# Value products in reverse order, matmuls of zeros at the start and in ten waits, a pinned norm broadcast, pinned weight splits and GpSimd subtractions in halves

## The chip, the cores and the metric

The kernel runs on one core of one Trainium2 chip. A core has TensorE (PE, matrix products, with weight loads shown apart as PEld), VectorE (DVE), ScalarE (ACT), GpSimd (POOL) and a queue on SyncE (SP) that issues the DMA transfers here. Each engine works through its own instructions strictly in the order in which they were emitted and waits where an operand is not there. The metric is the device time of one execution in microseconds (us); lower is better.

## The reference

Two transformer layers over two streams of 256 tokens, the context stream (s=0) and the latent stream (s=1), with model width 1024. Each layer is a half-step SwiGLU feed-forward stage, a token-mixing stage and another half-step feed-forward stage, and each stage reads a modulated RMS norm of the streams:

```
def modulate(h, g, shift, scale):
    return rms_norm(h, g) * (1 + scale) + shift

def swiglu(h, wi, wo):
    gt, up = jnp.split(h @ wi, 2, axis=-1)
    return (jax.nn.silu(gt) * up) @ wo

for l in range(DEPTH):            # DEPTH = 2
    x  = x  + HALF * mod_l[2] * swiglu(modulate(x,  ...), ffn1_wi[l], ffn1_wo[l])
    xc = xc + HALF * mod_c[2] * swiglu(modulate(xc, ...), ffn1_wi[l], ffn1_wo[l])
    y_l, y_c = token_mix(modulate(x, ...), modulate(xc, ...), w_in[l], ...)
    x  = x + mod_l[5] * (y_l @ w_out[l])
    x  = x + HALF * mod_l[8] * swiglu(modulate(x, ...), ffn2_wi[l], ffn2_wo[l])
    # the context stream likewise, in the first layer only
```

`token_mix` projects the normed streams with one input matrix and splits the columns among three groups of heads: A, a bidirectional mLSTM; B, six heads of latent attention; C, six heads of windowed attention with a sink logit per head. An attention head is a softmax over score tiles and a product of the probabilities with the values. The outputs of the groups are joined and projected by `w_out`.

## The kernel before, in words

All large products are made nearly exact in a fast format: a weight `w` is split into a high part (`ACT`, `AF.Copy` into float32r) and a low part (`w` minus the high part, on DVE or on POOL, `split`, L241 to L251), a stream likewise, and `mm3` (L237) adds three products for each pair of tiles. Other products (statistics, broadcasts, attention scores from full floats, value products) are plain float32; in the trace each of those shows as two records.

The feed-forward stages (`ffn`, L443) take 22 column blocks `j`; `up` makes gate and up products over eight row tiles `kt`, `down` (L574) the output rows. At the very start, in `norm_first` (L394), the statistics of the inputs are taken, and `ada_block` (L304) makes the eight blocks of the first modulation, one for each `kt`; a row tile of the normed stream (`modulate`, L377) needs its block. In between stages a `Norm` object (L98) carries the norm of a stream: `sq` squares each finished row tile on ACT (L111) and adds the squares on POOL (L115), `stats` sums over partitions with one-column products and raises to the power -1/2 on POOL (`rsqrt`, L375), `bcast` spreads the result over partitions with two small products, and `mods` applies it, row tile by row tile: DVE L383, then ACT L386 and DVE L387 for even row tiles, ACT L390, L391 and POOL L392 for odd ones.

The mixing stage (`mix`, L1182) is cut into some hundred small units (generators): projections (`chunk`, `proj`; names k1, k2, cq, o, v, q1, q2), attention tiles (`attend`, L607), mLSTM heads, the output projection. A table `PLAN` gives each group of units a place and a step, the units are sorted by it, and `run` starts `add` of them per round and keeps up to `width` of them active (`CFG`). Tables `CHP` and `OPT` choose which engine does a split or a copy. Within all of this a list scheduler with its own model of times decides the final order on each engine.

In `attend`, a tile takes scores into PSUM, the row maximum (DVE L629 or L632, with L633 for the sink), the exponential (ACT L637), the sum with the sink's term (DVE L643), the reciprocal (L644), the normalisation (POOL L651, DVE L649 or ACT L647), four transposes (PE L657), their copies, and for the last tile of a pair of heads the value product (PE L671), two heads beside each other in the array.

Of the kernel before, what the change touches and what calls it, by code (L numbers as in the profile page):

```python
# [10 lines left out]
F32 = mybir.dt.float32  # L11
F32R = mybir.dt.float32r
AF = mybir.ActivationFunctionType
ALU = mybir.AluOpType
# [23 lines left out]
def dper(nj):  # L38
# [18 lines left out]
]  # L57
CFG = [(2, 9), (1, 10)]
CHP = [
    {"k1": 1, "cq": 1, "o": 1, "k2": 0, "v": 1, "q1": 1, "q2": 0},  # L60
    {"k1": 1, "cq": 0, "o": 1, "k2": 0, "v": 0, "q1": 0, "q2": 1},
]
OPT = [
# [3 lines left out]
     "rbcq": 1, "sqfi": 2},  # L67
# [14 lines left out]
]  # L82
MODS = {0: (0, 0, 0, 2, 1, 1, 0, 0), 2: (0, 0, 0, 1, 1, 1, 1, 1), 3: (0, 0, 0, 2, 1, 1, 0, 0)}
# [14 lines left out]
class Norm:  # L98
# [19 lines left out]
    def stats(self):  # L118
        b, p = self.b, self.begin()
        self.R = b.ps((P, 258), "R1" if self.s else "R0")  # L120
        for tt in range(2):
            for t in self.sqs:
                b.mm(self.R[:, 256 + tt:257 + tt], t[:, tt * P:(tt + 1) * P], b.ones, t is self.sqs[0],
                     t is self.sqs[-1])
        self.r = b.sm(2, "sn")
        b.rsqrt(self.r, self.R[:, 256:258], 1.0 / D, 2)
        b.phase = p
# [14 lines left out]
class Builder:  # L142
    def __init__(self, tc, a, es):
# [17 lines left out]
        self.layer = 2  # L161

# [71 lines left out]
    def mm(self, out, lhsT, rhs, start, stop):  # L234
        self.nc.tensor.matmul(out, lhsT, rhs, start=start, stop=stop)  # L235
# [6 lines left out]
    def split(self, raw, alloc, shape, pool=False):  # L242
# [10 lines left out]
    def setup(self):  # L253
# [18 lines left out]
        nc.vector.memset(self.ones, 1.0)  # L272
        self.nhalf = c.tile([P, 16], F32, name="nhalf")
# [103 lines left out]
    def modulate(self, l, i, s, kt, R, hh, hl):  # L377
# [7 lines left out]
        if kt % 2 == 0:  # L385
            nc.scalar.activation(hh[kt][:, u], t, AF.Identity, bias=sh)  # L386
            nc.vector.scalar_tensor_tensor(hl[kt][:, u], t, sh, hh[kt].bitcast(F32)[:, u],  # L387
                                           op0=ALU.add, op1=ALU.subtract)
        else:
            nc.scalar.activation(t, t, AF.Identity, bias=sh)  # L390
            nc.scalar.activation(hh[kt][:, u], t, AF.Copy)  # L391
            nc.gpsimd.tensor_tensor(hl[kt][:, u], t, hh[kt].bitcast(F32)[:, u], op=ALU.subtract)  # L392

    def norm_first(self):  # L394
# [6 lines left out]
        qs = []  # L401
        for s in range(2):
# [7 lines left out]
        for s in range(2):  # L410
            self.phase = "norm000"
            u = slice(s * 256, s * 256 + 256)
            for tt in range(2 * s, 2 * s + 2):
                for k in range(2):
                    self.mm(st[tt], qs[s][:, k, tt % 2 * P:(tt % 2 + 1) * P], self.ones, k == 0, k == 1)
# [1053 lines left out]
```

## Time and profile before

| | |
|---|---|
| time, median of 3 runs (lowest to highest) | 1780.37 us (1778.57 to 1781.23) |
| the profiled execution: its own time | 1779.1 us |
| its span, from first to last instruction | 1777.4 us |
| PE busy | 1735.6 us, 98% of the span |
| PEld, DVE, ACT, POOL busy | 84%, 68%, 40%, 17% |
| mean granted clock of TensorE | 0.994 |
| DMA | 252.34 MB, mean 142 GB/s |

PE is busy nearly all the time. Two things are to be read of it: where it waits, and at which clock it works. The profile lists the clock that was granted, 1.00 being the upper of its two levels (2.4 GHz) and 0.50 the lower (1.2 GHz). A matmul's listed duration includes its pipeline, so the pace of a series is read from the starts.

### The profile page before, as it was taken

How to read it: one execution, taken by the hardware profiler on the slowest of the kernel's cores; microseconds unless marked ns; L12 is line 12 of the kernel's file. 1: busy time of each engine (PE TensorE's matmuls, PEld its weight loads, DVE VectorE, ACT ScalarE, POOL GpSimd, SP SyncE). 2: the span in 40 equal slices, each digit the busy share in tenths (PEclk: the TensorE clock that was granted, in tenths of full speed). 3: DMA queues.
4: the chain of work that ended last, by engine and by line, in shares of the span. 5: the costliest groups of instructions: out<-in, count | busy, mean ns of one | idle time of the engine just before them, and what ended most of it. 6: DMA issues, size and time to landing. Idle time of an engine off the chain costs nothing. (4 is left out here: it accounts for less than half of the span.)

```text
span 1777.4 us, 27225 instructions
## 1 busy us (share of the span) xinstructions
PE 1735.6 (98%) x10048; PEld 1494.9 (84%) x10048; DVE 1215.6 (68%) x2836; ACT 705.0 (40%) x1340; POOL 309.2 (17%) x350
## 2 busy tenths in 40 slices
PE   7999999999999999999999999999999999999999
PEld 5788888899977799888888898888888887699999
DVE  5699687957778856986853469785334588755555
ACT  3422222235566664222222353222322566554443
POOL 2100000025344680000000030000000466340000
PEclk9999999999999999999999999999999999999999
DMA  8656455632110145574633346654223241045654
GB/s 335 208 185 223 150 191 182 213 97 81 61 37 25 48 140 197 183 237 147 197 103 91 118 135 210 210 170 154 82 76 123 69 126 45 23 129 162 210 158 150
DMA packets 99590, 252.34 MB, mean 142 GB/s; under 512 B 12289, under 2 KB 16769, under 8 KB 98433
## 3 DMA queue, kind: packets, MB, share of 16 engines
q1 hardware_dynamic: 99456, 250.60, 43.5%
q8 instruction: 79, 1.29, 0.3%
q14 instruction: 55, 0.44, 0.1%
HBM read 249.51 MB, written 1.05 MB: 141 GB/s over the span
## 5 line engine op out<-in xcount | busy, mean ns | idle before, releaser
L246 ACT ACTIVATE w<-raw 128x1024 fp32r<-128x1024 f32 (+2 forms) x366 | 344.7, 944 | 573.9 <-PE tr L235 232.6
L250 DVE TENSOR_TENSOR w<-raw,w 128x1024 fp32r<-128x1024 f32 (+1 forms) x330 | 354.2, 1074 | 204.5 <-ACT w L246 202.9
L235 PE MATMUL sc<-h,w 128*128 128x512 f32 (+1 forms) x1428 | 355.3, 365 | 0.0
L235 PE MATMUL sc<-big,w 128*128 128x256 f32 (+1 forms) x1488 | 328.8, 340 | 1.8 <-ACT big L386 1.1
L235 PE MATMUL tr<-h,w 128*128 128x512 f32 (+1 forms) x1128 | 298.2, 373 | 1.2 <-DVE h L387 0.6
L235 PEld LDWEIGHTS sc<-h,w 128*128 128x128 f32 x1428 | 251.1, 190 | 44.0 <-issue 1.6
L235 PEld LDWEIGHTS sc<-big,w 128*128 128x128 f32 x1488 | 245.0, 191 | 32.0 <-issue 1.8
L235 PE MATMUL tr<-big,w 128*128 128x256 f32 (+1 forms) x1128 | 243.3, 326 | 0.0
L235 PEld LDWEIGHTS tr<-h,w 128*128 128x128 f32 x1128 | 204.9, 190 | 38.3 <-DVE h L387 0.8
L235 PE MATMUL ps<-h,w 128*128 128x256 f32 (+1 forms) x1404 | 216.3, 312 | 0.6 <-DVE x L436 0.6
L235 PEld LDWEIGHTS ps<-h,w 128*128 128x128 f32 x1404 | 195.4, 191 | 16.1 <-DVE x L436 0.9
L248 POOL TENSOR_TENSOR w<-raw,w 128x1024 fp32r<-128x1024 f32 (+2 forms) x36 | 84.1, 2340 | 688.4 <-ACT w L246 686.1
L235 PEld LDWEIGHTS tr<-big,w 128*128 128x128 f32 x1128 | 182.5, 191 | 17.8
L235 PE MATMUL ps<-big,w 128*128 128x512 f32 (+1 forms) x864 | 185.5, 372 | 0.7 <-DVE x L436 0.7
L352 DVE CUSTOM_DVE_ANT_0 hold<-a,a 128x512 f32<-128x512 f32 x256 | 177.7, 694 | 4.0 <-DMA a<-ada_t 4.0
L352 DVE CUSTOM_DVE_ANT_0 a<-a,a 128x512 f32<-128x512 f32 x256 | 175.8, 687 | 3.7
L235 PEld LDWEIGHTS ps<-big,w 128*128 128x128 f32 x864 | 153.6, 188 | 29.3 <-DVE x L436 1.0
L235 PE MATMUL ps<-w,h 128*128 128x256 f32 (+1 forms) x1152 | 169.3, 300 | 7.7 <-POOL h L392 2.1
L235 PEld LDWEIGHTS ps<-w,h 128*128 128x128 f32 x1152 | 151.2, 195 | 15.9 <-POOL h L392 2.3
L467 DVE TENSOR_TENSOR a<-a,tr 128x512 f32<-128x512 f32 (+1 forms) x90 | 54.3, 603 | 149.3 <-ACT a L466 78.3
L466 ACT ACTIVATE a<-sc 128x512 f32<-128x512 f32 (+1 forms) x91 | 48.3, 531 | 271.4 <-PE sc L235 266.4
L436 DVE SCALAR_TENSOR_TENSOR x<-ps,gate,x 128x256 f32<-128x256 f32 x150 | 68.2, 479 | 67.2 <-PE ps L235 66.9
(253 smaller groups left out, 1582.5 us busy)
## 6 DMA issues: line engine op xcount, KB each, us to landing
raw<-wi SPq DMA_DIRECT2D x176, 512.0 KB, 4.2
a<-ada_t SPq DMA_DIRECT2D x256, 256.0 KB, 4.6
raw<-wo SPq DMA_DIRECT2D x128, 320.0 KB, 3.0
raw<-w_out SPq DMA_DIRECT2D x24, 512.0 KB, 3.4
big<-ada_s SPq DMA_DIRECT2D x8, 1024.0 KB, 10.9
raw<-wo SPq DMA_DIRECT2D x8, 512.0 KB, 3.6
raw<-win_q SPq DMA_DIRECT2D x8, 512.0 KB, 4.1
a<-crow SPq DMA_DIRECT2D x12, 256.0 KB, 6.4
```

Source lines behind the costliest of these rows:

```text
L235: self.nc.tensor.matmul(out, lhsT, rhs, start=start, stop=stop)
L246: nc.scalar.activation(h, raw, AF.Copy)
L248: nc.gpsimd.tensor_tensor(l, raw, h.bitcast(F32), op=ALU.subtract)
L250: nc.vector.tensor_tensor(l, raw, h.bitcast(F32), op=ALU.subtract)
L352: nc.vector.tensor_tensor_reduce(out=w if s else junk, in0=w, in1=self.cb[s, hf], scale=1.0, scalar=0.0, op0=ALU.mult, op1=ALU.add, accum_ ...
L436: self.nc.vector.scalar_tensor_tensor(xs, ps, self.gate[l][:, s, i, d:d + 1], xs, op0=ALU.mult, op1=ALU.add)
L466: nc.scalar.activation(sg, pg, AF.Silu)
L467: nc.vector.tensor_tensor(sg, sg, pu, op=ALU.mult)
```

## The change

What it does, in the code:

- **Zeros at the start.** `norm_first` issues products of zeros (128x512, plain float32) into a bank that nobody reads: six at the very start, two behind the statistics of stream 0, one of 256 columns behind those of stream 1 (`FIRST`).
- **Zeros in ten waits.** `pad` issues products of zeros into the bank that the next real product overwrites (or adds to), at ten places (`PADS`): behind the statistics of two norms, ahead of one row tile of the first feed-forward stage of layer 1, and ahead of the transposes of seven attention tiles, where they read the sum of the exponentials and so start when it is there. All 29 issues of zeros are nine at the start, two of 256 columns behind statistics, two in the feed-forward stage and 16 of 128 columns.
- **Pinned order.** In the norms between stages, the next ordinary product may not be moved ahead of the broadcast (`first`); the zeros behind the statistics come ahead of it. The high parts of the k2 weights may not be moved ahead of the last ACT step of stream 0's norm (`late`).
- **Halves.** Where POOL makes the low part of a weight, it does so in two halves along the row tiles: 36 instructions become 74, with some splits moved between DVE and POOL (`CHP`).
- **The sink's sum** (L643) becomes a `tensor_scalar` with the sink's term as its per-partition scalar.
- **Value products and gate transposes** go through their tiles in reverse order.
- **Tables** `PLAN`, `CFG`, `OPT`, `CHP` get new entries, which reorder units of both mixing stages.

```
+FIRST = {0: (512,) * 6, 1: (512, 512), 2: (256,)}
+PADS = {"at0C0201": 384, "at0C1000": 512, "at0C1010": 384, "at1C0000": 768, "at1C1011": 128, "at1C1201": 256,
+     "at1C1210": 384, "r010": 384, "r100": 256, "up1007": 384}
...
-    {"k11": (-1, 4.1), "k10": (0, 1), "n1": (2, 0), "k20": (1.8, 0.6), "k21": (3.7, 0.6), "B10": (13, 2), "cq": (9,
+    {"k11": (-1, 4.1), "k10": (0, 1), "n1": (2, 0), "k20": (8, 0.9), "k21": (4.6, 0.6), "B10": (13, 2), "cq": (9,
...
         b.rsqrt(self.r, self.R[:, 256:258], 1.0 / D, 2)
+        b.pad(self.R[:, 0:256], f"r{self.l}{self.i}{self.s}", True, last, whole=True)
...
     def mm(self, out, lhsT, rhs, start, stop):
-        self.nc.tensor.matmul(out, lhsT, rhs, start=start, stop=stop)
+        i = self.last = self.nc.tensor.matmul(out, lhsT, rhs, start=start, stop=stop)
+        if self.first is not None:
+            self.behind(i, self.first)
+            self.first = None
...
+    def pad(self, out, key, start=False, after=None, x=None, whole=False):
+        n = PADS.get(key, 0)
+        w = out.shape[1]
+        if n and start:
+            n = max(1, n // w) * w
+        for k in range(0, n, w):
+            m = min(w, n - k)
+            i = self.nc.tensor.matmul(out[:, 0:m], self.zero.to_broadcast([P, P]), (self.zero if x is None else
+                                      x[:, 0:1]).to_broadcast([P, m]), start=start, stop=whole)
+            if after is not None:
+                self.behind(i, after)
+        return n > 0
...
-        nc.scalar.activation(h, raw, AF.Copy)
+        i = nc.scalar.activation(h, raw, AF.Copy)
+        if late:
+            self.behind(i, self.after["a"])
         if pool:
-            nc.gpsimd.tensor_tensor(l, raw, h.bitcast(F32), op=ALU.subtract)
+            m = shape[1] // 2
+            for v in (slice(0, m), slice(m, shape[1])):
+                nc.gpsimd.tensor_tensor(l[:, v], raw[:, v], h.bitcast(F32)[:, v], op=ALU.subtract)
...
+        warm(0)
         for s in range(2):
...
+            warm(1 + s, last)
             for tt in range(2 * s, 2 * s + 2):
                 self.mm(R[:, tt * P:(tt + 1) * P], r[:, tt:tt + 1].to_broadcast([P, P]), self.ident, True, True)
...
                                         nx[0].bcast()
+                                        self.first = self.last
...
-                nc.vector.tensor_tensor(st[:, 2:3], st[:, 2:3], st[:, 3:4], op=ALU.add)
+                nc.vector.tensor_scalar(st[:, 2:3], st[:, 2:3], st[:, 3:4], None, op0=ALU.add)
...
             for kt in range(nkt):
+                if kt == 0:
+                    self.pad(tr[:, 0, :], f"at{self.layer}{label[3]}{s}{heads[0]}{b}{qi}", True, None, st[:, 2:3], True)
                 nc.tensor.transpose(tr[:, kt, :], p[:, kt * P:(kt + 1) * P], self.ident)
...
-                for kt in range(nkt):
-                    for b2, h2 in enumerate(heads):
-                        nc.tensor.matmul(pv[64 * b2:64 * b2 + 64, :], V(kt, h2), pts[b2][kt // 2][:, kt % 2, :],
-                                         start=kt == 0, stop=kt == nkt - 1, tile_position=(0, 64 * b2))
+                for kt in reversed(range(nkt)):
+                    for b2 in (1, 0):
+                        nc.tensor.matmul(pv[64 * b2:64 * b2 + 64, :], V(kt, heads[b2]), pts[b2][kt // 2][:, kt % 2, :],
+                                         start=kt == nkt - 1, stop=kt == 0, tile_position=(0, 64 * b2))
```

**PE at the very start.** Before, these rows lead to the first product of the first feed-forward stage (sc_216 on h_4, row tile 0); `ps_189`, `ps_242` and `ps_286` are the modulation blocks 0, 1 and 2, the one-column products are statistics, the `ident,sn` products the broadcast.

```order
L316 MATMUL ps_189<-big_119,a_3_126 32x256 x8
L235 MATMUL hold_163<-ident,sn_165 128x128
L235 MATMUL sc_161<-ones,w_29_172 128x1 x2
L235 MATMUL sc_162<-ones,w_29_172 128x1 x2
L235 MATMUL ps_189<-sel,a_32_198 128x2 x2
L235 MATMUL hold_163<-ident,sn_165 128x128 x2
L316 MATMUL ps_242<-big_240,a_3_126 32x256 x8
L235 MATMUL ps_242<-sel,a_50_251 128x2 x2
L316 MATMUL ps_286<-big_284,a_3_126 32x256 x8
L235 MATMUL sc_216<-h_4_143,w_40_224 128x512
```

In the change the same place on PE reads as follows (`ps_169` takes the zeros; six more of them and the statistics of stream 0 stand ahead of these rows).

```order
L442 MATMUL ps_169<-a_27_168 128x512 x2
L349 MATMUL ps_202<-big_119,a_3_128 32x256 x8
L460 MATMUL sc_163<-ones,w_31_183 128x1 x2
L460 MATMUL sc_164<-ones,w_31_183 128x1
L242 MATMUL hold_165<-ident,sn_167 128x128 x2
L460 MATMUL sc_164<-ones,w_31_183 128x1
L442 MATMUL ps_169<-a_27_168 128x256
L242 MATMUL hold_165<-ident,sn_167 128x128 x2
L242 MATMUL ps_202<-sel,a_34_211 128x2 x2
L349 MATMUL ps_257<-big_255,a_3_128 32x256 x8
L242 MATMUL ps_257<-sel,a_52_266 128x2 x2
L242 MATMUL sc_230<-h_4_145,w_42_238 128x512
```

Block 2 no longer stands ahead of the first product: it comes behind the first twelve of them.

**PE at the end of the first feed-forward stage of layer 0.** Before, twelve `down` products (`ps_3465`, `ps_3496`) stand between the statistics of stream 0 and their broadcast, and six (`ps_3507`) behind it, ahead of the k1 projection. These rows are the last of the twelve and what follows.

```order
L235 MATMUL ps_3496<-big_3100,w_630_3192 128x256
L235 MATMUL ps_3496<-big_3101,w_629_3191 128x256
L235 MATMUL hold_3413<-ident,sn_3418 128x128 x2
L235 MATMUL ps_3507<-big_3100,w_629_3191 128x256
L235 MATMUL ps_3507<-big_3100,w_630_3192 128x256
```

In the change the zeros and the broadcast follow the statistics directly.

```order
L127 MATMUL hold_3429<-ones,a_652_3341 128x1
L127 MATMUL hold_3429<-ones,a_666_3417 128x1
L258 MATMUL hold_3429<-zero 128x256
L242 MATMUL hold_3429<-ident,sn_3434 128x128 x2
L242 MATMUL ps_3482<-big_3116,w_631_3207 128x256
```

All eighteen `down` products now stand between the broadcast and the k1 projection. The order at the two later boundaries (from layer 0 to layer 1, and into the mixing stage of layer 1) changes in the same way, the second of them without zeros.

**POOL in the mixing stage of layer 1.** The rows with `h_` are the last steps of stream 1's norm (L392, in the change L425), those with `sq_` powers of norms of heads.

```order
L392 TENSOR_TENSOR h_2502_12820<-a_2643_13448,h_2501_12819 128x256
L375 TENSOR_TENSOR sq_13453<-sq_13453,nhalf 128x2
L375 TENSOR_TENSOR sq_13479<-sq_13479,nhalf 128x6
L392 TENSOR_TENSOR h_2506_12824<-a_2650_13473,h_2505_12823 128x256
L232 TENSOR_TENSOR a_2645_13457<-a_2645_13457,sq_13479 128x576
```

In the change:

```order
L425 TENSOR_TENSOR h_2504_12874<-a_2637_13484,h_2503_12873 128x256
L408 TENSOR_TENSOR sq_13515<-sq_13515,nhalf 128x2
L425 TENSOR_TENSOR h_2508_12878<-a_2646_13509,h_2507_12877 128x256
L408 TENSOR_TENSOR sq_13583<-sq_13583,nhalf 128x6
L239 TENSOR_TENSOR a_2648_13519<-a_2648_13519,sq_13583 128x576
```

The last step of the norm now stands ahead of the 128x6 power.

## Rows read from the trace of the kernel before

**Rows 1.** Busy us (and instructions) of PE, PEld, DVE, ACT, POOL; granted clock; DMA.

```profile
390.00:404.00 14.00, 12.56 (x97) 11.58 (x96) 11.72 (x27) 9.26 (x23) 11.64 (x15) 1.00 0.43 141
404.00:411.00 7.00, 7.00 (x31) 7.00 (x31) 3.48 (x7) 2.78 (x8) 3.85 (x5) 0.51 0.22 77
...
547.50:551.00 3.50, 3.50 (x14) 1.93 (x14) 2.34 (x10) 3.03 (x11) 2.13 (x5) 0.52 0.02 7
...
1020.00:1035.50 15.50, 13.90 (x108) 12.89 (x108) 13.58 (x29) 10.70 (x28) 11.80 (x14) 1.00 0.30 99
1035.50:1039.00 3.50, 3.50 (x18) 3.50 (x18) 2.22 (x5) 1.51 (x5) 2.90 (x4) 0.51 0.50 147
...
1390.00:1428.00 38.00, 33.83 (x243) 31.27 (x241) 28.71 (x71) 23.79 (x60) 22.70 (x27) 1.00 0.23 72
1428.00:1431.50 3.50, 3.32 (x13) 2.95 (x14) 1.26 (x3) 2.37 (x7) 3.42 (x4) 0.51 0.57 185
...
1581.50:1585.50 4.00, 3.63 (x17) 3.36 (x18) 4.00 (x10) 3.94 (x11) 1.92 (x3) 0.57 0.09 33
```

**Rows 2.** PE in order of time at the start: start us, us, instructions merged, [idle before].

```profile
10.31 1.87 PE L235 MATMUL tr<-ones,w 128*128 128x1 f32 x8 [10.31 <-DVE w L409]
...
24.05 1.93 PE L316 MATMUL ps<-big,a 128*32 128x256 f32 x16
25.91 1.22 PE L235 MATMUL sc<-h,w 128*128 128x512 f32 x2
...
28.63 0.64 PE L235 MATMUL tr<-h,w 128*128 128x512 f32 x2
...
31.46 0.62 PE L316 MATMUL ps<-big,a 128*32 128x256 f32 x2
...
36.74 1.93 PE L316 MATMUL ps<-big,a 128*32 128x256 f32 x30
```

**Rows 3.** ACT in order of time at the start.

```profile
22.94 0.89 ACT L386 ACTIVATE h<-a,mod 128x256 fp32r<-128x256 f32 x2
```

**Rows 4.** PE, ACT and POOL in order of time, into the mixing stage of layer 0.

```profile
397.58 1.68 PE L235 MATMUL ps<-big,w 128*128 128x256 f32 x12
...
401.41 1.04 ACT L246 ACTIVATE w<-raw 128x1024 fp32r<-128x1024 f32 x1
...
404.76 6.63 PE L235 MATMUL ps<-w,h 128*128 128x304 f32 x26
...
407.65 1.41 POOL L392 TENSOR_TENSOR h<-a,h 128x256 fp32r<-128x256 f32 x2
```

**Rows 5.** PE in order of time, a broadcast right behind its statistics (end of layer 1's mixing).

```profile
1579.65 0.71 PE L235 MATMUL sc<-ident,sn 128*128 128x128 f32 x4 [1.04 <-POOL sn L375]
```

**Rows 6.** PE's waits from 1394 to 1436 us: total, times, longest.

```profile
PE ps L235 <- POOL h L392: 2.1, 1, 2.1
```

**Rows 7.** POOL in order of time, mixing stage of layer 1, first half.

```profile
1424.29 2.40 POOL L375 TENSOR_TENSOR sq<-sq,nhalf 128x6 f32<-128x6 f32 x1 [1.15 <-DVE sq L374]
```

**Rows 8.** DVE lines L643 and L633: duration ns min/median/max, first and last start.

```profile
L643 DVE TENSOR_TENSOR sa<-sa x36: 129/150/2075, 542.6 to 1546.9; 128x1 f32<-128x1 f32 x36
...
L633 DVE TENSOR_SCALAR sa<-sa,sink x36: 192/202/215, 534.9 to 1544.8; 128x1 f32<-128x1 f32 x36
```

**Rows 9.** POOL, DVE and PE in order of time, mixing stage of layer 1.

```profile
1506.98 2.34 POOL L248 TENSOR_TENSOR w<-raw,w 128x1024 fp32r<-128x1024 f32 x1
...
1507.26 2.08 DVE L643 TENSOR_TENSOR sa<-sa 128x1 f32<-128x1 f32 x1
...
1509.82 0.47 PE L235 MATMUL ps<-big,kSA 96*128 96x256 f32 x2 [1.16 <-DVE sa L633]
```

**Rows 10.** PE in order of time, mixing stage of layer 0.

```profile
546.38 0.63 PE L657 MATMUL tr<-ident,a 128*128 128x128 f32 x4 [1.48 <-DVE w L968]
```

**Rows 11.** The chain that ended last, in order of time: start us, us, what.

```profile
1494.89 0.86 PE sc L235 x2
```

**Rows 12.** PE's groups of instructions: busy us, mean ns, idle before.

```profile
L671 PE MATMUL ps<-a,big 128*64 128x256 f32 x240 | 40.0, 396 | 1.2 <-DVE a L224 0.6 <-DVE tot L1125 0.5
```

More of the change, by code (lines that the diff above doesn't have):

```diff
@@ L161, in __init__ @@
         self.layer = 2
+        self.last = self.first = None
+        self.after = {}
     def nm(self, s):
@@ L240, in mm3, with split @@
         self.mm(out, wh, xl, False, last)
-    def split(self, raw, alloc, shape, pool=False):
+    def split(self, raw, alloc, shape, pool=False, late=False):
         nc = self.nc
@@ L272, in setup @@
         nc.vector.memset(self.ones, 1.0)
+        self.zero = c.tile([P, 1], F32, name="zero")
+        nc.vector.memset(self.zero, 0.0)
         self.nhalf = c.tile([P, 16], F32, name="nhalf")
@@ L390, in modulate @@
             nc.scalar.activation(t, t, AF.Identity, bias=sh)
-            nc.scalar.activation(hh[kt][:, u], t, AF.Copy)
+            i = nc.scalar.activation(hh[kt][:, u], t, AF.Copy)
             nc.gpsimd.tensor_tensor(hl[kt][:, u], t, hh[kt].bitcast(F32)[:, u], op=ALU.subtract)
+        if s == 0:
+            self.after["a"] = i
     def norm_first(self):
@@ L401, in norm_first, with warm @@
         qs = []
+        wz, wp = self.a2([P, 512]), self.ps(tag="ps")
+        nc.vector.memset(wz, 0.0)
+        def warm(k, after=None):
+            for n in FIRST.get(k, ()):
+                i = nc.tensor.matmul(wp[:, 0:n], wz[:, 0:P], wz[:, 0:n], start=True, stop=True)
+                if after is not None:
+                    self.behind(i, after)
+        warm(0)
         for s in range(2):
@@ L414, in norm_first @@
                 for k in range(2):
-                    self.mm(st[tt], qs[s][:, k, tt % 2 * P:(tt % 2 + 1) * P], self.ones, k == 0, k == 1)
+                    last = nc.tensor.matmul(st[tt], qs[s][:, k, tt % 2 * P:(tt % 2 + 1) * P], self.ones, start=k == 0,
+                                            stop=k == 1)
                 self.rsqrt(r[:, tt:tt + 1], st[tt], 1.0 / D, 1)
+            warm(1 + s, last)
             for tt in range(2 * s, 2 * s + 2):
@@ L452, in ffn, with up @@
         tags = ("sc", "tr")
-        def up(js, wts, pgs, streams_, kts=range(KT)):
+        def up(js, wts, pgs, streams_, kts=range(KT), key=None):
             self.phase = f"ffn{l}{i}"
@@ L457, in up @@
             for kt in kts:
+                began = self.pad(pgs[js[0]][0][:, c0:c1], f"{key}{kt}", kt == 0) and kt == 0
                 for j in js:
@@ L461, in up @@
                         self.mm3(pgs[j][g][:, c0:c1], wh[:, kt % 4, g, :], wl[:, kt % 4, g, :],
-                                 hh[kt][:, c0 + t0:c1 + t0], hl[kt][:, c0 + t0:c1 + t0], kt == 0, kt == KT - 1)
+                                 hh[kt][:, c0 + t0:c1 + t0], hl[kt][:, c0 + t0:c1 + t0],
+                                 kt == 0 and not (began and j == js[0] and g == 0), kt == KT - 1)
         def act(pg, pu, gh, gl, n):
@@ L592, in chunk, with proj @@
             self.dma(w, self.a["win_" + name][l, :, q:q + nk, :])
-            wh, wl = self.split(w, self.w4, [P, nk, W], pool=CHP[self.layer][name] > (q == 0))
+            wh, wl = self.split(w, self.w4, [P, nk, W], pool=CHP[self.layer][name] > (q == 0),
+                                late=name == "k2")
             out += [(wh[:, k, :], wl[:, k, :]) for k in range(nk)]
         return out, W
-    def proj(self, ch, h, tts):
+    def proj(self, ch, h, tts, key=None):
         (hh, hl), (cw, W) = h, ch
@@ L601, in proj @@
             wh, wl = cw[kt]
+            began = self.pad(pss[0], f"{key}{kt}", kt == 0) and kt == 0
             for tt, ps in zip(tts, pss):
                 th, tl = hh[kt][:, tt * P:(tt + 1) * P], hl[kt][:, tt * P:(tt + 1) * P]
-                self.mm3(ps, th, tl, wh, wl, kt == 0, kt == KT - 1)
+                self.mm3(ps, th, tl, wh, wl, kt == 0 and not (began and ps is pss[0]), kt == KT - 1)
         return pss
@@ L984, in u_gates @@
             self.phase = f"gates{l}"
-            src = self.ps((36, NT), "gtr")
-            for tt in range(4):
-                nc.tensor.transpose(src[:, tt * P:(tt + 1) * P], self.gp[:, tt, k, :], self.ident)
+            src = self.ps((P, NT), "gtr")
+            for tt in reversed(range(4)):
+                nc.tensor.transpose(src[:, tt * P:(tt + 1) * P], self.gpw[tt][k], self.ident)
             yield
@@ L1030, in u_gates @@
         trg = self.ps((P, 4, 3, 36), "gtr")
-        for tt in range(4):
-            for k, src in enumerate((nat[1], nat[2], ae)):
+        for k, src in ((2, ae), (1, nat[2]), (0, nat[1])):
+            for tt in reversed(range(4)):
                 nc.tensor.transpose(trg[:, tt, k, :], src[:, tt * P:(tt + 1) * P], self.ident[:36, :36])
@@ L1215, in mix @@
         nc.vector.memset(self.vA[:, :, :, 64:65], 1.0)
-        self.gp = self.lt([P, 4, 2, 36], "gp")
-        nc.vector.memset(self.gp, 0.0)
+        gp = self.lt([P, 384], "gp")
+        nc.vector.memset(gp, 0.0)
+        self.gp = gp[:, 0:288].rearrange("p (t k c) -> p t k c", t=4, k=2)
+        self.gpw = [[gp[:, 72 * t + 36 * k:72 * t + 36 * k + P] for k in range(2)] for t in range(4)]
         store = {}
```

24 lines of the change are left out of this document (13 added, 11 removed), and 21 rows, old and new, of tables (OPT, PLAN).

## The prediction

> **What bounds the kernel now.** I read the busy times first: PE is busy for 98% of the span, so everything else counts only where it makes PE wait or work slowly. Then I cut the span into stretches with the granted clock beside them. The long feed-forward stages are full and at clock 1.00. What is lost lies in a few places. Five stretches show about half the clock [rows 1]: 404 to 411 us (0.51), 547.5 to 551 (0.52), 1035.5 to 1039 (0.51), 1428 to 1431.5 (0.51) and 1581.5 to 1585.5 (0.57). In them PE is busy for 20.95 us of 21.5, so it does at the lower level (1.2 GHz) what would take half the time at the upper. Each stretch follows one in which PE waited in short pieces: 12.56 us busy of 14.0 ahead of the first, 13.90 of 15.5 ahead of the third, 33.83 of 38.0 ahead of the fourth [rows 1]. Lost at half speed: 7.0 × 0.49 = 3.4 us in the first and 1.7 in each of the others.
>
> The start is a sixth such place, though the clock column says 1.00 there, so I read the pace in the timeline of PE [rows 2]. From 25.91 to 28.63 us six products of 512 columns start, one per 0.45 us; from 28.63 to 31.46 twelve, one per 0.236. The modulation block at 24.05 takes 1.93 us for 16 records; from 36.74, 30 records take the same 1.93. So up to 28.6 us PE ran at about half pace, and ahead of 10.31 it did nothing.
>
> **The change part by part.** The sums are made against the profiled execution, 1779.1 us (its span of 1777.4 and 1.7 around it). That is 1.3 below the median of the runs shown. About 3.6 us, 0.2%, can be told from no change.
>
> *The start (A).* A product of zeros with 512 columns in plain float32 is two records, as in the chain, where two took 0.86 us [rows 11]; at half pace 1.72. Six take 5.2 to 10.3 us. They can start once the zeros are written, at about 2.8 us (an estimate: the memsets of 0.3 us each that stand ahead), and must be over by 10.31, when the first statistics are released [rows 2]. In the trace, dense work from 24.05 on ran 4.6 us before the pace doubled. Six zeros with such a ramp end at 2.8 + 4.6 + 3.3 × 0.86 = 10.2. So they just fit; all at half pace they end at 13.1 and cost 2.8.
> Then the order. The operand of the first product is ready at 22.94 + 0.89 = 23.83 [rows 3], but block 2 holds PE until 25.9. In the change block 2 comes behind twelve products. From 23.83, eighteen products (18 × 0.236) and one block (0.97) end at 29.05; before, this is reached at 31.46. That is 2.4 us. Block 1 at full pace would bring the operand a microsecond earlier still, and the clock may also fall back in the thin work between 12 and 22 us. Value −2.4, bounds −4.1 and +2.8. From there on PE was busy without a gap of any size, so the lead stays.
>
> *Into the mixing stage of layer 0 (B).* Before, twelve products cover the wait for the power on POOL, at 0.12 us each (12 start from 397.58 to the broadcast's start about 1.5 later) [rows 4]. Now the broadcast follows directly. The price is on view at 1579.65, where it already does: PE waits 1.04 us [rows 5]. The one product of 256 zeros (0.43) lies inside this wait. In return the norm's steps start 1.44 us earlier behind eighteen products that need none of them, and the k2 split of 1.04 us on ACT (401.41) goes behind them [rows 4]. POOL's last step, which ended at 407.65 + 1.41 = 409.06, comes at about 406.6, before PE can be there. So the short waits ahead of 404 (1.44) go, and if the clock holds, the 3.4 of the stretch behind: −1.44 − 3.4 + 1.04 = −3.8. In the stretch 26 products of 304 columns took 6.63 us [rows 4], so it was work and not waiting. The k2 split is now late by two to three microseconds; the 48 k1 products (6 us at full clock) cover it. Bounds: 0 if the clock falls all the same, −4.8 if also the new wait is hidden.
>
> *The rest of that stage (C).* The stretch at 547.5 (−1.7) follows the longest wait of the stage, 1.48 us [rows 10]. Ten products of 128 zeros stand ahead of transposes; each is a quarter of 0.86, so 2.15 together, of which I let 1.2 be exposed. −1.7 − 1.5 + 1.2 = −2.0, bounds −3.2 and +2.2 (all zeros exposed, nothing cured). The tables reorder units here, and no row prices that; I take it at nothing, and its bounds from the waits of the stretch around it, within these.
>
> *Into layer 1 (D).* 15.5 − 13.90 = 1.6 of waits and 1.7 of clock, against 1.04 for the new wait and 0.64 for 384 zero columns in the up products: −1.6, bounds −3.3 and +1.7.
>
> *Into the mixing stage of layer 1 (E).* Waits of 4.17 us [rows 1], of which 2.1 is one, for a step of the norm on POOL [rows 6]. That step stood behind a 128x6 power of 2.40 us [rows 7]; in the change it stands ahead of it. The other 2.1 I count half. With 1.7 of clock and 1.04 for the new wait: −2.1 − 1.05 − 1.7 + 1.04 = −3.8, bounds −5.9 and 0.
>
> *The rest of it (F).* The sink's sum on 128x1 took 0.15 us in the median and 2.08 at most [rows 8]. The longest starts at 1507.26 and ends at 1509.34, with a subtraction on POOL that ran from 1506.98 to 1509.32; behind it PE stood for 1.16 us [rows 9]. L633, a `tensor_scalar` on the same shape with a pointer to its scalar, never took more than 0.215 in 36 [rows 8]. So the new form does not wait, and halves shorten what other DVE steps wait to about 1.2. −1.2, against 6 × 0.215 = 1.3 of zeros, half exposed: −0.5, bounds −2.5 and +3 (a new order no row prices).
> The Trainium skill, page "SBUF — State Buffer", section "Who interferes with whom", says that `tensor_scalar` can also enter a mode that takes the port shared with GpSimd, and that the loser is blocked for the whole instruction. By that rule the new form would stall as the old one did and the sum would be 1.2 higher, 1766.2; the 36 rows of L633 say otherwise, and I follow them.
>
> *At nothing:* the reversed gate transposes (same number), a wider `CFG`, and the halves' own cost. POOL takes 0.7 for 128x256 [rows 4] against 2.34 for four times that [rows 9], so an extra instruction costs about (4 × 0.7 − 2.34) / 3 = 0.16; 38 of them make 6 us on an engine that is busy 17%, hidden in its idle time. Were all exposed, 6 us.
> The end of layer 1's mixing keeps its order and its stretch at 1581.5.
>
> Sum: −2.4 − 3.8 − 2.0 − 1.6 − 3.8 − 0.5 = −14.1, so 1765.0.
>
> **The rivals.**
> *The clock falls elsewhere.* The waits are no longer the same, but some remain (1.04 behind each statistics, most of it uncovered at E, and those in the attention tiles). If four new stretches of 3.5 us appear, 4 × 1.7 = 6.8 comes back: about 1772. For it: the falls before came after waits of 1.4 to 4.2 us in pieces, which is little. Against it: the zeros stand in just such places.
> *More comes out.* The start's operand a microsecond earlier and the waits in both attention parts gone (A −4.1, C −3.2, F −2.5, E −5): 1758.
> *It does not do what it says.* New waits in the reordered attention parts eat up all but 2 of the 14.1: 1777. The tables touch some 20 groups of units, and no row prices them.
> *Slower: the reversed value products.* A product now begins with the tile that was copied last, where before it began with the first. There are 18 (240 records: twelve of 16, six of 8) [rows 12]. Now they wait 1.2 us in all. If each waited 1.1 for its last copy, with PE idle meanwhile, that is 19.8: 1784.8. It decides from (14.1 + 3.6) / 18 = 0.98 each. Against it: the same copies were needed before for the later half, so only the overlap of the first half is lost, and the scheduler places other products ahead.
>
> **How the numbers follow.** The forecast, 1761 to 1769, 0.55; falling elsewhere, 1769 to 1775, 0.20; more, 1757 to 1761, 0.13; all eaten up, 1776 to 1782, 0.07; slower, 0.05. Leaving out the last two and a little of the rest, the range is 1757 to 1775. Faster by over 0.2% (below 1776.8): 0.55 + 0.20 + 0.13 and a little of the fourth, 0.89. Within 0.2%: 0.06. Slower: 0.05.
>
> **What would show it.** A: PE starts at about 3 us with zeros, the first 512-column product at 24 us or before, and the pace is 0.236 from its first product. B, D, E: the broadcast directly behind the statistics with a wait of about 1 us, clock 1.00 from 400 to 415, from 1015 to 1040 and from 1395 to 1435 (all some microseconds earlier), no wait over 1 us for the norm's last step on POOL. C and F: no L643 over 0.3 us, no stretch at half clock in the attention parts. The stretch at 1581.5 is still there. It would be wrong if the zeros at the start run past 10.3 us, if new stretches at half clock appear, or if PE waits more than before in the attention parts.

## The result and the profile after

The changed kernel takes 1770.1 us (median of 5 runs, 1769.9 to 1774.2) where the kernel before took 1780.4: 0.9948 of its time, 95% interval 0.9936 to 0.9960. It is faster, by 9 to 10 us where 14.1 were forecast; the range held it. First the head of its page: the span and, for each engine, busy us, share and instructions.

```profile
span 1767.9 us, 27368 instructions
PE 1729.5 (98%) x10106; PEld 1494.7 (85%) x10106; DVE 1213.3 (69%) x2827; ACT 711.8 (40%) x1355; POOL 316.2 (18%) x384
```

PE is busy 6.1 us less, with 17.0 us of zeros added, so other work on PE became shorter by 23. Part of it is the clock, for which the forecast had terms; 10.4 us are the value products (40.0 us busy before [rows 12], 29.7 now), for which it had none.

Read from the trace, the change is in four points a little other than described above. Zeros are issued at nine places, not ten: the entry `at1C0000` names a tile of the context stream in layer 1, which that layer does not compute, so the zeros stand in six attention tiles and not seven. (The expectations below count the entries, ten.) The low parts on POOL are 76 instructions and not 74 (38 splits in two halves each). The first gate transposes not only change their order, they also become wider (128 columns instead of 36). And the zeros behind the statistics into layer 1 came with a different order of the products that follow, which is taken up at e11_two.

Next, stretches of the span, with columns as in [rows 1].

```profile
20.50:27.50 7.00, 6.13 (x23) 4.49 (x16) 3.92 (x10) 1.29 (x3) 0.96 (x1) 0.51 1.02 418
390.00:404.00 14.00, 13.25 (x99) 12.16 (x98) 10.10 (x25) 8.43 (x23) 11.28 (x16) 1.00 0.28 95
404.00:411.00 7.00, 6.55 (x50) 6.33 (x50) 5.48 (x13) 3.74 (x10) 3.65 (x4) 1.00 0.32 96
541.00:548.00 7.00, 5.52 (x43) 4.11 (x44) 6.35 (x23) 6.70 (x24) 1.67 (x5) 1.00 0.29 96
1011.00:1030.50 19.50, 17.89 (x135) 16.32 (x134) 16.89 (x33) 12.66 (x30) 13.45 (x15) 1.00 0.27 90
1030.50:1034.50 4.00, 4.00 (x22) 4.00 (x22) 1.19 (x4) 1.40 (x4) 2.11 (x3) 0.57 0.85 249
1380.00:1420.00 40.00, 38.26 (x285) 36.22 (x284) 29.39 (x70) 27.68 (x67) 27.01 (x32) 1.00 0.22 70
1570.00:1577.00 7.00, 5.92 (x26) 5.66 (x27) 5.61 (x12) 4.53 (x12) 3.24 (x4) 0.51 0.14 46
```

Against [rows 1]: the half-clock stretches into both mixing stages and at 547 us are gone. The one into layer 1 stands, and that at the end of layer 1's mixing is twice as long.

To see where the time went I cut every profile at four marks that all kernels have: the starts of the one-column statistics of stream 0 into layer 0's mixing, into layer 1 and into layer 1's mixing, and of stream 1 at the end of that. (Before: 396.77, 1027.00, 1395.65 and 1576.45 us.) The five lengths, and the us from 60 us on in which the granted clock was about half (without the last 2 us of the span):

| kernel | median us | ratio to before | start | mixing 0 and on | into layer 1 and on | mixing 1 | rest | half clock |
|---|---|---|---|---|---|---|---|---|
| before | 1780.4 | 1 | 396.8 | 630.2 | 368.7 | 180.8 | 200.9 | 20.5 |
| changed | 1770.1 | 0.9948 | 395.9 | 624.6 | 370.3 | 175.1 | 202.0 | 10.2 |
| e5_same | 1770.3 | 0.9958 | 395.5 | 624.5 | 370.3 | 175.1 | 202.0 | 10.2 |
| e1_fwd | 1776.7 | 0.9982 | 396.5 | 629.9 | 368.8 | 176.7 | 202.8 | 13.7 |
| e2_rev | 1784.9 | 1.0021 | 395.1 | 631.2 | 370.2 | 186.9 | 201.8 | 44.4 |
| e3_nofirst | 1772.3 | 0.9960 | 396.5 | 625.9 | 371.8 | 175.6 | 202.2 | 20.5 |
| e4_nopads | 1770.7 | 0.9948 | 396.5 | 625.7 | 367.6 | 177.2 | 201.8 | 17.1 |
| e6_tabrev | 1780.1 | 1.0015 | 396.9 | 634.7 | 370.2 | 179.7 | 201.8 | 44.4 |
| e7_tail | 1770.2 | 0.9957 | 395.6 | 624.5 | 370.3 | 175.1 | 201.9 | 6.8 |
| e8_nopin | 1774.3 | 0.9973 | 395.6 | 628.5 | 367.8 | 178.1 | 201.9 | 20.5 |
| e9_whole | 1771.4 | 0.9963 | 397.0 | 626.0 | 368.8 | 175.4 | 202.0 | 13.7 |
| e10_sink | 1770.4 | 0.9958 | 396.3 | 627.5 | 368.8 | 175.0 | 201.7 | 13.7 |
| e11_two | 1768.3 | 0.9944 | 396.0 | 624.5 | 367.2 | 175.0 | 201.9 | 10.2 |
| e12_gates | 1771.6 | 0.9965 | 398.5 | 624.6 | 370.3 | 175.1 | 201.8 | 10.2 |

The kernels ran on several chips, so each ratio is to the kernel before on the same chip: its median was 1778.9 us on the chip of e1 to e4 and on that of e5 to e8, and 1778.0 on that of e9 to e12. The medians themselves can be compared only within such a group. The intervals of the ratios reach 0.001 to 0.0013 to either side, and the changed kernel itself came out at 0.9948 and at 0.9958 (e5_same): a difference of 0.001 says nothing. The lengths are of one profile each, and a profile can lie at the edge of its kernel's runs: those of e2_rev (1787.0 us) and e6_tabrev (1785.1) are the slowest of twelve. The 9.5 us between the two profiles are: start −0.9, mixing 0 −5.6, into layer 1 +1.6, mixing 1 −5.7, rest +1.1.

### The profile page after: what moved, and what is told of

Its sections match the earlier page's. It is cut to its first block, busy times and chain, and to the rows that moved or that the text cites. A ratio compares the mean times of both kernels' runs of the same rounds, so it can differ in the third digit from the quotient of the medians.

```text
span 1767.9 us, 27368 instructions
## 1 busy us (share of the span) xinstructions
PE 1729.5 (98%) x10106; PEld 1494.7 (85%) x10106; DVE 1213.3 (69%) x2827; ACT 711.8 (40%) x1355; POOL 316.2 (18%) x384
## 5 line engine op out<-in xcount | busy, mean ns | idle before, releaser
L279 POOL TENSOR_TENSOR w<-raw,w 128x512 fp32r<-128x512 f32 (+1 forms) x76 | 97.0, 1300 | 696.6 <-ACT w L273 695.9
L242 PE MATMUL ps<-w,h 128*128 128x256 f32 (+1 forms) x1152 | 163.6, 294 | 4.3 <-DVE a L233 1.1
L242 PEld LDWEIGHTS ps<-w,h 128*128 128x128 f32 x1152 | 147.0, 191 | 10.7 <-issue 2.5
```

The lines of the kernel that those rows point to most:

```text
L242: i = self.last = self.nc.tensor.matmul(out, lhsT, rhs, start=start, stop=stop)
L279: nc.gpsimd.tensor_tensor(l[:, v], raw[:, v], h.bitcast(F32)[:, v], op=ALU.subtract)
```

## The experiments

**Forward value products (e1_fwd).**

```
-                for kt in reversed(range(nkt)):
-                    for b2 in (1, 0):
+                for kt in range(nkt):
+                    for b2, h2 in enumerate(heads):
```

> The changed kernel with the value products in their old order (forward, head 0 first). Theory P: in the new order a value product starts only when its last tile is copied and then runs as one burst in which the two heads work beside each other; in the old order it starts early, in pieces (2 records, later 6), and the heads no longer pair. Then the value products' busy time goes back from 29.7 to about 40 us and the time rises by 3 to 8 us, to 1773 to 1778. Rival W: the early start was overlap, and the gain of the mixing stages came from clock, zeros and tables alone: 1768 to 1771.

Measured 1776.7 us, 0.9982 (0.9973 to 0.9992): theory P. Below are the value products by group in the changed kernel, then in this one (busy us, mean ns, idle before).

```profile
L725 PE MATMUL ps<-a,big 128*64 128x256 f32 x240 | 29.7, 386 | 1.2 <-ACT a L235 0.7 <-DVE a L231 0.5
```

```profile
L725 PE MATMUL ps<-a,big 128*64 128x256 f32 x240 | 40.3, 391 | 0.3 <-ACT a L235 0.3
```

The same 240 records take 40.3 us without a wait, or 29.7 us with 1.2 us of waits. The timeline of PE shows why. In the changed kernel a value product is one burst:

```profile
566.41 1.08 PE L725 MATMUL ps<-a,big 128*64 128x256 f32 x8
567.42 0.74 PE L242 MATMUL sc<-big,w 128*128 128x512 f32 x2
...
583.02 1.95 PE L725 MATMUL ps<-a,big 128*64 128x256 f32 x16
```

In e1_fwd it comes in pieces, with other products between:

```profile
565.82 0.65 PE L725 MATMUL ps<-a,big 128*64 128x256 f32 x2
566.40 0.44 PE L242 MATMUL ps<-vA,a 128*128 128x65 f32 x2
...
568.29 1.08 PE L725 MATMUL ps<-a,big 128*64 128x256 f32 x6
569.29 0.71 PE L242 MATMUL sc<-big,a 128*128 128x260 f32 x2
```

Eight more records lengthen the burst by 1.95 − 1.08 = 0.87, 0.109 us each: the two heads' records, one in each half of the array, run beside each other (in the trace they start in pairs 0.006 us apart, a pair every 0.216 us). The first two records of e1_fwd are one head alone and hold PE for 0.58 us (565.82 to 566.40); the other six take 1.00, because only four of them find a partner and the last two run alone, 0.216 us apart. That is 1.58 us for what takes 1.01 (566.41 to 567.42). The Trainium skill, page "TensorE: Matmul & The Clock Gate", section "Part 3: Packing small matmuls — row/col tiling", says that products at different tile positions run concurrently in the same array; the trace agrees, with 0.109 us a record in pairs against 0.216 alone, and here those that pair are those that stand next to each other. In layer 0 the products are 25.2 us busy here and 18.0 in the changed kernel, and that part is 5.3 us longer. In layer 1 they are 15.1 against 11.7, but that part is only 1.6 us longer, which can as well be the one stretch at half clock that came at 1461 us: PE, busy for 4.6 us more there, waits 3.0 us less (8.1 against 11.1). So the shorter products pay in layer 0; that they do in layer 1 is not shown.

**Reversed value products alone (e2_rev), and with the new tables (e6_tabrev).** The first is the kernel before with the lines above turned; the second also takes `PLAN`, `CFG`, `CHP` and `OPT` from the change.

> The kernel before with the reversed value products alone. Theory P: their busy time falls from 40 to about 30 us and the time by 3 to 8 us, to 1772 to 1777. Rival W: nothing or slower, 1779 to 1785.

> The kernel before with the reversed value products and the new tables, and nothing else (no zeros, no pins, whole subtractions, old form of the sink's sum, gate transposes forward). Theory P (the gain of the mixing stages is that of the value products, and the tables place other work ahead of them so that their wait is covered): both stages keep most of it, value products about 30 us busy with under 2 us of waits ahead, 1770 to 1775. Rival Z (zeros, pins, halves and the sink's sum are needed): 1776 or more, waits or stretches at half clock as in the kernel before with the reversed products alone.

Measured 1.0021 (1.0008 to 1.0034) for e2_rev and 1.0015 (1.0004 to 1.0026) for e6_tabrev. P was right on the busy time (32.5 and 33.1 us, from 40.0) and wrong on the time; the times are those of W and Z. In e2_rev PE waits for the products' last copies, as the slower rival of the prediction said:

```profile
PE ps L671 <- DVE a L224: 2.8, 2, 2.1
PE ps L671 <- ACT a L228: 2.4, 2, 1.7
```

In e6_tabrev the tables cut these waits to 1.2 us, but both kernels spend 44 us at half clock from 60 us on, against 20.5 before. One row of each kind in e2_rev, a norm and an attention part:

```profile
402.00:409.00 7.00, 7.00 (x31) 7.00 (x31) 3.80 (x7) 3.09 (x9) 3.92 (x5) 0.51 0.25 86
...
1542.00:1546.00 4.00, 3.93 (x15) 3.41 (x16) 3.83 (x15) 2.95 (x11) 1.86 (x4) 0.57 0.00 0
```

In these two profiles 24 us more at half clock cost 12, more than the 7.5 and 6.9 us of shorter products gain. They are the slowest of their runs, though. The mean granted clock of all twelve runs is 0.990 and 0.989, against 0.992 for the kernel before on the same chips, which by itself comes to some 4 and 5 us (an estimate: the difference of the clocks times the span). So the clock takes back much of the gain in the other runs too, and 3 to 4 us of the loss stay unexplained there.

Both theories had a part: the gain is P's, and it stays only with what rival Z named. Which of those edits is needed is open. On the same chip the changed kernel (e5_same) is 9.8 us faster than e6_tabrev, while each of them undone alone, below, costs at most 4.

**No zeros at the start (e3_nofirst), none in the waits (e4_nopads), and the changed kernel again (e5_same).**

```
-FIRST = {0: (512,) * 6, 1: (512, 512), 2: (256,)}
+FIRST = {}
```

> The changed kernel without the nine issues of zeros at the start. Theory T (from about 30 us on the start is set by transfers of the modulation tables, for which PE waits 2.0 us in the changed kernel): PE is slower up to 28 us and waits less behind it, at most 1.0 us is lost, 1770 to 1771.2. Rival C (the clock sets the start): 2.4 us or more are lost, 1772.5 to 1774.

> The changed kernel without zeros in the ten waits. Theory Z (they keep the clock up): two to four stretches at half clock come back, 1.7 us each, less some 1 us that the zeros cost: 1772.5 to 1776, and the stretches show in the granted clock. Rival N (the shorter waits alone keep it up, the zeros only cost): 1768.5 to 1770.5 and no new stretch.

> The changed kernel once more, as the measure for the other kernels of this chip, and for where its clock falls. If the places of the half-clock stretches are set by the instructions alone, the stretches of the first profile come again (about 20.5, 1030.5 and 1570 us, the last for 6.8 us). If chance has a part, others appear with the same order of instructions. Time 0.994 to 0.996 of the kernel before either way, about 1768 to 1772.

e4_nopads (`PADS = {}`) gave 0.9948 (0.9936 to 0.9960) and e5_same 0.9958 (0.9945 to 0.9970): the zeros in the waits are worth nothing that was measured. Two stretches at half clock came back without them (543 and 1540 us), as Z said, and the time is rival N's, about (1770.7). They save half clock (10.2 against 17.1 us) and cost PE's time and, into layer 1, order: that part is 2.7 us shorter without them. e3_nofirst gave 0.9960 (0.9947 to 0.9972): its 1772.3 us lie between its two theories, but beside e5_same's 0.9958 no loss is shown. In its profile (1773.9 us) the start is 0.6 us longer only, as T says. The rest of the profile's loss lies where its instructions are the same: from 142 us on it has the same order on every engine as the changed kernel. Here is one place in both, a wait of transposes in layer 0's mixing, first the changed kernel:

```profile
542.03 0.63 PE L711 MATMUL tr<-ident,a 128*128 128x128 f32 x4 [1.43 <-DVE w L1022]
543.11 0.50 PE L242 MATMUL sc<-qSA,kSA 96*128 96x256 f32 x2 [0.46 <-DVE qSA L231]
```

and then e3_nofirst, with its stretches behind:

```profile
542.68 0.63 PE L711 MATMUL tr<-ident,a 128*128 128x128 f32 x4 [1.43 <-DVE w L1022]
543.76 0.79 PE L242 MATMUL sc<-qSA,kSA 96*128 96x256 f32 x2 [0.46 <-DVE qSA L231]
...
543.50:547.50 4.00, 3.74 (x19) 3.21 (x21) 2.18 (x9) 4.00 (x15) 0.46 (x1) 0.57 0.20 78
1396.50:1400.50 4.00, 4.00 (x23) 4.00 (x23) 2.85 (x7) 2.50 (x7) 2.35 (x4) 0.57 0.25 78
```

The same instructions and waits of 1.43 and 0.46 us: the clock held in one and fell in the other. e5_same fell where the changed kernel had. What differs in e3_nofirst is when all this comes, 0.65 us later. A fall is thus not a property of one wait alone. The part into layer 1 shows it in steps: 368.8 us with no fall (e1_fwd, e9_whole, e10_sink), 370.3 with 3.4 us at half clock, 371.8 with 6.8, with the same order of instructions there.

**Zeros at the end of layer 1's mixing (e7_tail).**

```
-     "at1C1210": 384, "r010": 384, "r100": 256, "up1007": 384}
+     "at1C1210": 384, "r010": 384, "r100": 256, "up1007": 384, "r121": 512, "up120": 256}
```

> The changed kernel with zeros at the end of layer 1's mixing too: one product of 256 columns in the wait for the last squares (0.94 us), two in the wait behind the last statistics (1.04 us); nothing else moves on any engine. Theory Z (zeros in a wait keep the clock): the 6.8 us at half clock from 1570 us shrink to 3.4 or none, 1.7 to 3.4 us gained, 1766.5 to 1769. Rival N (the clock falls with zeros too, since 1.1 us of waiting behind the broadcast stays): no gain, 1769.5 to 1772.

Z was right on the clock, N on the time (0.9957, 0.9945 to 0.9969). First the changed kernel's PE there:

```profile
1570.86 0.80 PE L242 MATMUL sc<-big,w 128*128 128x256 f32 x2 [1.11 <-ACT big L419]
...
1573.15 0.98 PE L242 MATMUL sc<-big,w 128*128 128x256 f32 x3 [0.22 <-DVE a L416]
```

and e7_tail's:

```profile
1567.92 1.14 PE L258 MATMUL sc<-zero 128*128 128x256 f32 x4 [0.25 <-DVE sn L407]
...
1570.61 0.50 PE L242 MATMUL sc<-big,w 128*128 128x256 f32 x2 [1.12 <-ACT big L419]
...
1572.90 0.98 PE L242 MATMUL sc<-big,w 128*128 128x256 f32 x3 [1.07 <-DVE a L416]
```

The half-clock stretch is 3.4 us instead of 6.8, but PE, now quicker through its first products, waits 1.07 us for the norm's next step on DVE where it waited 0.22. With the clock cured, the norm's steps set the pace.

**Pins, halves, the sink's sum, the gate transposes, two of the waits with zeros.** Each is the changed kernel with one edit undone. The list scheduler may then move other instructions as well: PE's order departs from the changed kernel's from 517 us on in e9_whole and from 564 us on in e10_sink. First the pins (e8_nopin):

```
-                                        self.first = self.last
...
-                                late=name == "k2")
+                                late=False)
```

The halves (e9_whole):

```
-            m = shape[1] // 2
-            for v in (slice(0, m), slice(m, shape[1])):
-                nc.gpsimd.tensor_tensor(l[:, v], raw[:, v], h.bitcast(F32)[:, v], op=ALU.subtract)
+            nc.gpsimd.tensor_tensor(l, raw, h.bitcast(F32), op=ALU.subtract)
```

The sink's sum (e10_sink):

```
-                nc.vector.tensor_scalar(st[:, 2:3], st[:, 2:3], st[:, 3:4], None, op0=ALU.add)
+                nc.vector.tensor_tensor(st[:, 2:3], st[:, 2:3], st[:, 3:4], op=ALU.add)
```

The zeros at the two places into layer 1 (e11_two):

```
-     "at1C1210": 384, "r010": 384, "r100": 256, "up1007": 384}
+     "at1C1210": 384, "r010": 384}
```

The gate transposes (e12_gates, the first of three places):

```
-            src = self.ps((P, NT), "gtr")
-            for tt in reversed(range(4)):
-                nc.tensor.transpose(src[:, tt * P:(tt + 1) * P], self.gpw[tt][k], self.ident)
+            src = self.ps((36, NT), "gtr")
+            for tt in range(4):
+                nc.tensor.transpose(src[:, tt * P:(tt + 1) * P], self.gp[:, tt, k, :], self.ident)
...
```

> The changed kernel without the pinned order (next products may go ahead of the broadcast, k2 splits not held back); zeros, tables and value products as changed. Forecast's step B: the short waits into both mixing stages come back, 1 to 4 us each, while the boundary into layer 1, where the changed kernel lost 1.6 us, gets up to 1.6 back: 1771 to 1775. Rival: what the pins gain at one place they lose at another, 1769 to 1771.

> The changed kernel with GpSimd's subtractions whole instead of in halves (38 instructions fewer on POOL). Theory H (while POOL subtracts, small DVE steps of the attention chains stand still; halves shorten this): waits of PE in the mixing stages grow and stretches at half clock come back, 1771.5 to 1775. Rival N (they lie off the path that sets the end): 1769 to 1771.

> The changed kernel with the sink's sum as a tensor_tensor again. Forecast's step F: steps of up to 1.3 us come back among the 36 (half of the 2.08 us seen before, since the subtractions are halved), and the time rises by 0.5 to 2.5 us, 1770.5 to 1773. Rival N: some sums are long, but none of them ends last, 1769.5 to 1770.5.

> The changed kernel without the zeros at the boundary into layer 1 (behind the statistics, and ahead of the last row tile); the other eight waits keep theirs. Without zeros anywhere in the ten waits this boundary gained 1.1 us on the kernel before, with them it lost 1.6. Theory A (the zeros cost more there than they keep): 1.5 to 3 us gained, 1766.5 to 1769, broadcast and first products earlier. Rival B (that difference was the place where the clock fell, not the zeros): 1769.5 to 1772, a longer stretch at half clock there.

> The changed kernel with the gate transposes in their old order and width; 16 records on PE change places within their groups, nothing else moves. Forecast: nothing, within 0.5 us of the changed kernel, 1769.5 to 1771. Rival (they shut a gap that the clock falls for): a new stretch at half clock near them and 1.7 us or more, 1771.5 or above.

*e8_nopin*, 0.9973 (0.9963 to 0.9984), as step B had it, and the one loss among these that is clear: eleven of its twelve runs are slower than every run of e5_same on the same chip (1771.0 at most). Mixing 0 is 3.9 us longer and mixing 1 3.1, with half clock at 405 and 545 (3.4 us each) and at 1399 (6.8), and the part into layer 1 2.5 us shorter. *e9_whole*, 0.9963 (0.9951 to 0.9976): its 1771.4 us lie between the two ranges, and no loss is shown, as rival N says; the 1.4 us that it is longer in mixing 0 goes with one stretch of 3.4 us at half clock that came there. *e10_sink*, 0.9958 (0.9946 to 0.9971): rival N; its profile has 2.9 us more in mixing 0, with 6.8 us at half clock at 543. The sum on DVE in the changed kernel, in e9_whole and in e10_sink (ns min/median/max):

```profile
L695 DVE TENSOR_SCALAR sa<-sa x36: 191/204/215, 539.0 to 1535.8; 128x1 f32<-128x1 f32 x36
```

```profile
L693 DVE TENSOR_SCALAR sa<-sa x36: 198/205/215, 539.8 to 1537.2; 128x1 f32<-128x1 f32 x36
```

```profile
L695 DVE TENSOR_TENSOR sa<-sa x36: 143/158/1243, 539.3 to 1537.5; 128x1 f32<-128x1 f32 x36
```

The new form never stood still: 16 of the 72 ran while POOL subtracted, seven of them beside whole subtractions, and all 72 took 0.215 us or less. The old one did, up to 1.24 us, until the subtraction ended (576.98 to 578.22, POOL's from 576.93 to 578.20), and it cost no time that was measured. The rule that the prediction quoted from the page "SBUF — State Buffer" of the Trainium skill, section "Who interferes with whom", that `tensor_scalar` can be blocked as well, found no case; the section says so only where the operands meet the mode's conditions, so the 72 do not speak against it.

*e12_gates*, 0.9965 (0.9952 to 0.9977): its 1771.6 us lie in the rival's range, but nothing changed in the part that holds the gates (624.6), as forecast; the profile's start was 2.6 us longer, with 13.7 us at half clock up to 40 us against 6.8, far ahead of the gates. *e11_two*, 0.9944 (0.9930 to 0.9957), theory A: the part into layer 1 is 3.1 us shorter at the same 3.4 us of half clock. That is not the zeros' own time alone (1.5 us of records): without them the scheduler puts six of the eighteen `down` products behind the first row tile, and PE waits 1.03 us there where it waited 1.61. Its five runs (1765.8 to 1768.8) lie below those of the other kernels on its chip (1769.1 at the lowest), but its interval overlaps the changed kernel's, so that it beats it is likely and not settled.

## Why the prediction was right, and where its steps were not

The table sets the two profiles beside each other by the steps of the prediction: PE's waits are the sums of its idle times, the zeros' time that of their records, before the arrow the kernel before and behind it the changed one. B ends at the second half of k1.

| step | forecast us | measured us | PE's waits | zeros | value products | at half clock |
|---|---|---|---|---|---|---|
| A | −2.4 | −0.9 | 12.4 → 8.1 | 10.1 | none | not listed → 6.8 |
| B | −3.8 | −3.2 | 1.7 → 1.2 | 0.7 | none | 6.8 → 0 |
| C | −2.0 | −2.4 | 7.5 → 9.8 | 2.7 | 24.3 → 18.0 | 3.4 → 0 |
| D | −1.6 | +1.6 | 1.6 → 1.6 | 1.5 | none | 3.4 → 3.4 |
| E, F | −4.3 | −5.7 | 11.8 → 11.1 | 2.0 | 15.7 → 11.7 | 3.4 → 0 |
| the end | 0 | +1.1 | 3.8 → 3.6 | none | none | 3.4 → 6.8 |

So the clock was read rightly for B, C and E. The waits were not: from B on they are 27 us where they were 26, instead of some microseconds fewer, and zeros took 7 us there where 2.5 had been counted. The value products, without a term, make up for it, so that the range held is in part luck. That PE waits more than before in layer 0's attention (C) is one of the signs by which the prediction said it would be wrong.

**A, the start** (−2.4; measured −0.9; between the medians of ten profiles with these zeros and four without, −0.5, and the two sets overlap, 395.5 to 398.5 and 395.1 to 396.9). Zeros began at 2.81 us as said and the first product came at 22.99 instead of 25.91. Two steps behind it failed. The clock fell back in the thin work (20.5 to 27.5), which I had named and not counted. And "from there on PE was busy without a gap, so the lead stays" was wrong, because more blocks moved than the one that I followed. PE, and one row of DVE, in order of time:

```profile
18.55 0.99 PE L242 MATMUL hold<-ident,sn 128*128 128x128 f32 x4 [2.19 <-POOL sn L408]
...
22.99 1.22 PE L242 MATMUL sc<-h,w 128*128 128x512 f32 x2 [0.38 <-ACT h L419]
...
32.68 0.35 DVE L358 TENSOR_SCALAR mod<-ps,ada_b 128x2 f32<-128x2 f32 x2 [7.90 <-PE ps L242]
...
33.13 1.07 PE L349 MATMUL ps<-big,a 128*32 128x256 f32 x16 [0.56 <-PE ps L242]
...
35.21 0.73 PE L242 MATMUL sc<-h,w 128*128 128x512 f32 x2 [0.48 <-ACT h L424]
...
52.16 1.07 PE L349 MATMUL ps<-big,a 128*32 128x256 f32 x16 [0.94 <-PE ps L242]
```

Blocks now stand behind each other, and one starts only when DVE has read an earlier one's result (33.03, then 33.13). The three waits are 1.98 us, and of the lead of 2.92 about 1 is left. That the banks cause it is argued from these rows; theory T's cause, transfers, is not shown: in e3_nofirst PE waits 0.2 us there, as T said, but the waits are the same 0.56, 0.48 and 0.94 us in e12_gates, whose start is 2.6 us longer.

**B and C** (−3.8 and −2.0; measured −3.2 to the second half of k1 and −2.4 behind it). B held. PE into layer 0's mixing, and last a row of the same step in layer 1:

```profile
395.89 0.95 PE L127 MATMUL hold<-ones,a 128*128 128x1 f32 x8
397.09 0.70 PE L258 MATMUL hold<-zero 128*128 128x256 f32 x2 [0.25 <-DVE sn L407]
397.87 0.71 PE L242 MATMUL hold<-ident,sn 128*128 128x128 f32 x4
398.34 2.58 PE L242 MATMUL ps<-big,w 128*128 128x256 f32 x18
...
402.03 2.51 PE L242 MATMUL ps<-w,h 128*128 128x304 f32 x16 [0.41 <-POOL h L425]
...
1396.89 2.49 PE L242 MATMUL ps<-w,h 128*128 128x304 f32 x16 [0.41 <-POOL h L425]
```

The broadcast comes 1.03 us behind the statistics (396.84 to 397.87), with the zeros in between; eighteen products cover the norm's first steps, and POOL's first step (L425, from 401.25) costs 0.41 us. Its last one ends at 408.0, where I had said 406.6, and PE does not wait for it. C has the right size from the wrong causes. I counted clock, waits and zeros, and took the reversal for a risk only. e1_fwd has no half clock in this part and is no faster than before there: what counts is 7.2 us of value products, 5.3 of them in time.

**D, into layer 1** (−1.6; measured +1.6) has the wrong sign. None of its terms came: the clock fell all the same, the old waits went but as many came behind the broadcast (0.21, 0.29 and 0.69 us, with 0.25 ahead of the zeros), and the zeros took 1.5 us, where I had counted 0.64 and the rest inside the wait. e11_two puts the price of the zeros, with the order that came with them, at 3.1 us. Without pins, too, the part is shorter (367.8, with no fall of the clock in it).

**E and F** (−4.3 together; measured −5.7). The norm's last step on POOL is ahead of the power as read from the order:

```profile
1415.81 0.95 POOL L425 TENSOR_TENSOR h<-a,h 128x256 fp32r<-128x256 f32 x1 [0.28 <-ACT h L424]
1417.03 2.23 POOL L408 TENSOR_TENSOR sq<-sq,nhalf 128x6 f32<-128x6 f32 x1 [0.28 <-DVE sq L407]
```

PE's wait of 2.1 us for it [rows 6] is gone; the 0.41 of the last PE row above is for another step, the first of stream 0's norm. These waits are gone in e1_fwd too, where PE waits 8.1 us in this part; in the changed kernel, whose value products are 3.4 us shorter than there, it waits 11.1. So the terms of E are borne out, and most of what the products became shorter in this layer shows up as waits. The sink's sum, −1.2 in F, gave nothing.

**The end of layer 1's mixing** kept its order and its stretch, as said, but that grew from 3.4 to 6.8 us, and the part behind the mark by 1.1.

**The rivals.** "The clock falls elsewhere" (1769 to 1775, with a chance of 0.20) has the measured time, and not the forecast's band of 1761 to 1769. Its mechanism did not come: of the three stretches that are left, two stand where they stood before and the third in the start, which ran at half pace before too. The slower rival is real, but in another kernel: in e2_rev the products wait up to 2.1 us. Two small sums of the prediction are off without consequence: "more comes out" adds up to 1758.9, not 1758, and an extra instruction of POOL to 0.15 us, not 0.16.

## What to carry to other kernels

Where two small products share the array, count what they gain by standing next to each other: starting the first one early, alone, can cost more than it overlaps. Weigh such an edit together with the order around it, since here it is worth 5 us with it and loses 4 without, and still 3 with the new tables alone. When a place's waits or clock are cured, look for what the next instruction waits for before counting the gain, and take a fall of the clock in a single profile as something that may come or go with the same instructions.

## What was not expected of the hardware

The stretches at half clock last 3.4, 6.8 or 10.2 us, and whether one comes is not set by the local waits alone: 1.43 and 0.46 us did and did not bring one. Records for two halves of the array take 0.109 us each side by side and 0.216 alone; two of one head alone held PE for 0.58. A `tensor_scalar` on 128x1 took at most 0.215 us in 72 cases, 16 of them beside a subtraction on POOL, a `tensor_tensor` beside one up to 1.24 and, before, 2.08 [rows 8].
